# Seven block products instead of eight in the up-projections of a decoder trunk in float32 parts

## The chip, the cores and the metric

The kernel runs on one core of one Trainium2 chip, in one launch. The metric is device time in microseconds (us), lower is better. TensorE (PE) does the matrix products into eight PSUM banks of 128 x 512 float32 numbers, VectorE (DVE) and ScalarE (ACT) do the elementwise work, GpSimd (POOL) a little of it, and SyncE (SP) issues the transfers between main memory and SBUF.

## The reference, cut to what matters

The trunk takes x of 512 tokens by 1024 features and runs two layers. Each layer is a feed-forward block, a mixer (a chunked spatial gating unit in the first layer, sparse attention in the second) and a second feed-forward block, each with a residual and a layer norm. The four feed-forward blocks hold the work that is changed:

```python
def swiglu(x, w1, w3, w2):
    return (jax.nn.silu(x @ w1) * (x @ w3)) @ w2      # w1, w3: 1024 x 2816, w2: 2816 x 1024

h = post_norm(h, 0.5 * swiglu(h, ...), ln_g, ln_b)
```

`x @ w1` and `x @ w3` are the up-projections, the product with `w2` is the down-projection.

## The kernel before, in words

Everything is kept feature-major for the up-projections: `xhi` and `xlo` hold x transposed (1024 features as eight k tiles of 128 partitions, 512 tokens). To keep float32 accuracy each operand is split into two float32r parts: `split` (lines 94 to 96) lets ACT copy the number into the high part and DVE subtract that from the number to give the low part. A product of two split operands takes three matmuls, high by high, high by low and low by high (`three`, lines 162 to 164).

The weights come as units of 128 x 1024 numbers (512 KB) in order of use. The class `Stream` loads a unit into one of two `raw` buffers (line 119, on SP), splits it into `whi` and `wlo` in a ring of five buffers (lines 95 and 96), and hands it out with `take`; `free` gives the buffer back and pumps the next split. One unit of an up-projection is 128 columns of w1 or w3, with all eight k tiles.

`ffn` (from line 261) goes over f = 0 to 21. For each f it makes two products with `feat`, one unit of w1 and one of w3, each of 8 x 3 = 24 matmuls of 512 tokens into a PSUM bank of tag A (tile `pab`), and then `gate` takes Silu on ACT and multiplies on DVE (line 271) into an `h` tile. In the three blocks that follow another layer directly or nearly so, the first four units are run in two halves of 256 tokens, so that TensorE can start before the last tokens have gone through the layer norm. Then `down` runs the token-major product with `w2` (line 236, tile `acc`, eight banks) and, in its last four row tiles, finishes one token tile after the other, each with its layer norm (`ln_tile`, lines 201 to 212), its transposes (line 221) and its split into `xhi` and `xlo`.

The tile framework's scheduler sets the order in which each engine meets its instructions; each engine then works strictly in that order, and waits on semaphores.

Of the kernel before, what the change touches and what calls it, by code (L numbers as in the profile page):

```python
# [17 lines left out]
P = 128  # L18
S = 512
# [20 lines left out]
NRAW = 2  # L40
# [8 lines left out]
NP = 16  # L49
# [5 lines left out]
def trunk_kernel(  # L55
    ctx: ExitStack,
    tc: tile.TileContext,
    x_tok: bass.AP,      # [NT, P, D]
    x_feat: bass.AP,     # [KD, P, S]
    wall: bass.AP,       # [units, P, 1024]  # L60
    lnp: bass.AP,        # [6, 2, D]
    sgu_ln: bass.AP,     # [2, 2, 1024]
    w_s: bass.AP,        # [P(s), 8, P(t)]
    b_s: bass.AP,        # [8, P(t)]
    rel: bass.AP,        # [32, 16]
    onehot: bass.AP,     # [32, S]
    cmp_w1: bass.AP,     # [2, 4, P, 1024]
    cmp_w2: bass.AP,     # [2, P, 2, 128]
    cmp_pe: bass.AP,     # [P, 2, 2, 16]
    cmp_b1: bass.AP,     # [P, 2, 2]  # L70
    out: bass.AP,        # [NT, P, D]
# [5 lines left out]
    work = pool("work", 2)  # L77
# [13 lines left out]
    xhi = const.tile([P, KD, S], F32R, name="xhi")  # L91
    xlo = const.tile([P, KD, S], F32R, name="xlo")
# [5 lines left out]
    # ---------------------------------------------------------------- weights  # L98
    class Stream:
        """Weight units in order of use: loaded ahead, split into two float32r parts ahead.  # L100

        A unit lives in the ring of NB buffers, or, for marked units, in a buffer of the phase's own pool, so that
        the ring can hold units of the next phase before this one ends.
        """

        def __init__(self, n):
            self.n = n
            self.loaded = self.cut = self.taken = self.freed = self.ring = 0
            self.raws, self.units, self.local = {}, {}, {}

        def load(self, upto):
            while self.loaded < min(upto, self.n):
# [12 lines left out]

        def pump(self, n=NB):
# [629 lines left out]
    for k in range(2):  # L756
        split(xhi[:, k, :], xlo[:, k, :], xf[:, k, :])
# [92 lines left out]
```

## Time and profile before

| what | value |
|---|---|
| median of three runs | 2102.51 us (2101.84 to 2107.32) |
| span of the profiled execution | 2100.6 us |
| fastest run less that span | 1.2 us |
| TensorE busy | 2076.1 us, 99% of the span |
| VectorE, ScalarE, GpSimd busy | 45%, 32%, 7% |
| mean granted TensorE clock | 0.996 of full speed |

The profile shows one execution, from its first to its last instruction; the device time of a run holds a little more than this span, here 1.2 us against the fastest run and 1.9 us against the median. The device time of the profiled execution itself is not listed apart. A matmul's duration in the profile includes its way through the array, which overlaps with the next one: what a matmul costs in a stream is the distance from its start to the next start.

### The profile page before, as it was taken

What the parts mean: (1) busy time and instruction counts of PE and PEld (TensorE: products, weight loads), DVE (VectorE), ACT (ScalarE), POOL (GpSimd) and SP (SyncE); (2) the same over time, 40 slices, a digit from 0 to 9 for tenths busy, and PEclk for the clock granted to TensorE, in tenths of its full rate; (3) what the DMA queues carried; (4) which work ended last, traced back from release to release, by engine and by line L of the source; (5) the groups of instructions that cost most, each with busy time, mean ns of one, the idle gap of its engine ahead of it and who ended that gap; (6) DMA issues with size and microseconds to landing.
All of it is one profiled execution on the core that took longest, in us unless ns stands there. A gap on an engine that the chain in (4) does not pass through costs nothing.

```text
span 2100.6 us, 24840 instructions
## 1 busy us (share of the span) xinstructions
PE 2076.1 (99%) x9859; PEld 1720.7 (82%) x9859; DVE 937.0 (45%) x1546; ACT 679.8 (32%) x1062; POOL 139.4 (7%) x249
## 2 busy tenths in 40 slices
PE   9999999999999999999999999999899999999998
PEld 7888888888889888888888888888777788888887
DVE  4322335456447322234733322336688864222234
ACT  4222232333233222222223222222578823222221
POOL 0000000000000000000000000000245500000002
PEclk9999999999999999999999999999899999999999
DMA  6223322333232322323472222222422114322221
GB/s 240 100 91 100 98 93 90 122 129 111 81 114 88 100 94 97 101 93 118 156 273 83 98 100 93 98 100 75 143 66 84 37 41 141 100 94 97 101 93 68
DMA packets 68804, 220.64 MB, mean 105 GB/s; under 512 B 7840, under 2 KB 12192, under 8 KB 67664
## 3 DMA queue, kind: packets, MB, share of 16 engines
q1 hardware_dynamic: 68688, 219.06, 31.3%
q8 instruction: 77, 1.26, 0.2%
q14 instruction: 39, 0.32, 0.0%
HBM read 212.70 MB, written 11.58 MB: 107 GB/s over the span
## 4 chain that ended last, share of the span: by engine, by line
PE 91%; DMA 3%; DVE 2%; ACT 2%; POOL 1%; issue 1%; SPq 0%; DVEq 0%; ACTq 0%; POOLq 0%
PE acc L236 29%; PE pab L162 15%; PE pab L163 15%; PE pab L164 15%; DMA raw<-in_wall_dram 2%; PE pv L163 2%; PE pv L164 2%; PE pv L162 2%; PE pu L164 1%; PE pu L162 1%; PE pu L163 1%; PE pt L658 1%; PE po L668 1%; PE po L669 1%; PE pt L221 1%; PE pss L585 1%
## 5 line engine op out<-in xcount | busy, mean ns | idle before, releaser
L96 DVE TENSOR_TENSOR wlo<-raw,whi 128x1024 fp32r<-128x1024 f32 (+1 forms) x343 | 417.3, 1218 | 518.9 <-ACT whi L95 491.9
L95 ACT ACTIVATE whi<-raw 128x1024 fp32r<-128x1024 f32 (+1 forms) x343 | 359.9, 1052 | 868.9 <-PE pab L163 571.5
L162 PE MATMUL pab<-xhi,whi 128*128 128x512 f32 (+1 forms) x1504 | 565.5, 376 | 0.5 <-ACT xhi L95 0.5
L164 PE MATMUL pab<-xhi,wlo 128*128 128x512 f32 (+1 forms) x1504 | 565.2, 376 | 0.6 <-DVE wlo L96 0.6
L163 PE MATMUL pab<-xlo,whi 128*128 128x512 f32 (+1 forms) x1504 | 565.0, 376 | 0.0
L162 PEld LDWEIGHTS pab<-xhi,whi 128*128 128x128 f32 x1504 | 283.2, 188 | 53.2 <-ACT xhi L95 1.9
L163 PEld LDWEIGHTS pab<-xlo,whi 128*128 128x128 f32 x1504 | 283.2, 188 | 51.9 <-DVE xlo L96 1.0
L164 PEld LDWEIGHTS pab<-xhi,wlo 128*128 128x128 f32 x1504 | 283.1, 188 | 51.6 <-DVE wlo L96 0.8
L236 PE MATMUL acc<-whi,shi 128*128 128x512 f32 x832 | 270.0, 390 | 0.0
L236 PE MATMUL acc<-whi,slo 128*128 128x512 f32 x832 | 269.9, 390 | 0.0
L236 PE MATMUL acc<-wlo,shi 128*128 128x512 f32 x832 | 269.3, 389 | 0.0
L236 PEld LDWEIGHTS acc<-whi,slo 128*128 128x128 f32 x832 | 156.2, 188 | 32.4
L236 PEld LDWEIGHTS acc<-wlo,shi 128*128 128x128 f32 x832 | 156.2, 188 | 32.2
L236 PEld LDWEIGHTS acc<-whi,shi 128*128 128x128 f32 x832 | 156.1, 188 | 31.9
L271 DVE TENSOR_TENSOR h<-tmp,pab 128x512 f32<-128x512 f32 x88 | 60.5, 688 | 272.5 <-PE pab L164 271.8
L96 DVE TENSOR_TENSOR slo<-h,shi 128x512 fp32r<-128x512 f32 x88 | 60.8, 691 | 206.5 <-ACT shi L95 206.5
L188 POOL TENSOR_TENSOR rs<-ve,half_neg 128x1 f32<-128x1 f32 x28 | 26.6, 951 | 1829.1 <-DVE ve L186 1829.1
L95 ACT ACTIVATE shi<-h 128x512 fp32r<-128x512 f32 x88 | 55.5, 631 | 246.2 <-PE acc L236 244.3
L607 POOL TENSOR_SCALAR p<-p,rc,gates 128x128 f32<-128x128 f32 (+3 forms) x128 | 76.4, 616 | 59.3 <-DVE rc L557 29.2
L594 ACT ACTIVATE p<-p,mn 128x128 f32<-128x128 f32 (+3 forms) x128 | 70.8, 554 | 9.8 <-DVE mn L591 9.4
L96 DVE TENSOR_TENSOR tl<-pt,th 128x512 fp32r<-128x512 f32 (+2 forms) x96 | 65.0, 682 | 12.8 <-ACT th L95 10.6
L591 DVE CUSTOM_DVE_ANT_0 p<-pss,u 128x128 f32<-128x128 f32 (+3 forms) x128 | 60.8, 483 | 9.6 <-PE pss L585 4.3
(144 smaller groups left out, 1955.3 us busy)
## 6 DMA issues: line engine op xcount, KB each, us to landing
raw<-in_wall_dram SPq DMA_DIRECT2D x339, 512.0 KB, 3.5
gb<-in_lnp_dram SPq DMA_DIRECT2D x6, 1024.0 KB, 7.5
skew_dr<-rev_dr SPq DMA_DIRECT2D x16, 320.0 KB, 8.2
cw<-in_cmp_w_dram SPq DMA_DIRECT2D x8, 512.0 KB, 6.3
u<-skew_dr SPq DMA_DIRECT2D x16, 256.0 KB, 3.6
k<-k_dr SPq DMA_DIRECT2D x32, 128.0 KB, 3.2
x_sb<-in_x_feat_dram SPq DMA_DIRECT2D x8, 256.0 KB, 5.2
x_sb<-in_x_tok_dram SPq DMA_DIRECT2D x4, 512.0 KB, 6.8
```

The source lines that it names most:

```text
L95: nc.scalar.activation(hi, src, AF.Copy)
L96: sub.tensor_tensor(lo, src, hi.bitcast(F32), op=ALU.subtract)
L162: nc.tensor.matmul(ps, ah, bh, start=first and i == 0, stop=False)
L163: nc.tensor.matmul(ps, ah, bl, start=False, stop=False)
L164: nc.tensor.matmul(ps, al, bh, start=False, stop=last and i == n - 1)
L188: nc.gpsimd.tensor_tensor(rs, ve, half_neg, op=ALU.pow)
L221: nc.tensor.transpose(pt[:, k * P:(k + 1) * P], x_sb[:, t, j * P:(j + 1) * P], ident)
L236: nc.tensor.matmul(acc[t][h], st[:, cs], mv[:, h * 512:(h + 1) * 512], start=s and i == 0, stop=e and i == 2)
L271: nc.vector.tensor_tensor(h, tmp, pb, op=ALU.mult)
L591: nc.vector.tensor_tensor_reduce(out=p[:, :nk], in0=ps[:, m0:m0 + nk], in1=ub[hh][:, S - nk:S], op0=ALU.add, op1=ALU.min, scale=-1.0, scal ...
L594: nc.scalar.activation(p[:, :nk], p[:, :nk], AF.Exp, bias=mn[:, hh:hh + 1], scale=-1.0, accum_out=sm[:, hh:hh + 1])
L607: nc.gpsimd.tensor_scalar(pr[i][:, :nk], pr[i][:, :nk], rc[:, i:i + 1], gates[:, br, h, qt:qt + 1], op0=ALU.mult, op1=ALU.mult)
```

## The change

The first two column pairs of a block (f = 0 and 1, `NPLAIN = 2`) are done as before. The other twenty are done two at a time by `double`. For a pair of columns f the two units (w1 and w3) and x are seen as 2 x 2 blocks: the weights by column (w1, w3) and by half of the features, x by half of the features and half of the tokens. The four block products of 128 columns by 256 tokens that eight smaller products made are now made by seven, after Winograd's form of Strassen's method. Each of the seven has 4 k tiles x 3 matmuls = 12 matmuls of 256 tokens. Sums of weight blocks (`prepare`, four adds of 128 x 512 per column pair, on VectorE) and of x blocks (`combos`, once per block) come before the products, sums of results after them.

`xhi` and `xlo` change their layout to four blocks [feature half + 2 x token half]; after the plain columns, block 2 is overwritten with the x sum `t4`. The ring of five split buffers stays; a `double` uses seven units of it. The raw buffers are two rings of three, by the parity of the unit. The `h`, `r`, `u`, `v`, `p` and `gb` tiles now share one pool of 24 slabs. Layer norms whose result feeds a feed-forward block keep an unsplit transposed copy (`keep`, one more ACT copy per half tile).

```diff
-NRAW = 2
+NRAW = 3
+NSUM = 4
+NSLAB = 24
+NPLAIN = 2
...
+        def plan_double(self):
+            a, b = self.unit, self.unit + 2
+            self.unit += 4
+            self.jobs += [("first", a), ("first", b), ("sum24", a), ("sum24", b), ("sum31", a), ("sum31", b),
+                          ("last", a, b)]
+        def load(self, n=None):
+            while self.loaded < (n or self.unit):
                 i = self.loaded
-                raw = stream.tile([P, 1024], F32, tag="raw", name=f"raw{i}", bufs=NRAW)
+                if i // 2 >= self.retired[i % 2] + NRAW:
+                    return
+                raw = stream.tile([P, 1024], F32, tag=f"raw{i % 2}", name=f"raw{i}", bufs=NRAW)
...
-                if i < 2:
-                    return      # the prologue loads the first two in halves
-                nc.sync.dma_start(raw, wall[i])
+                if i >= 2:
+                    nc.sync.dma_start(raw, wall[i])
...
+            if kind == "first":
+                split(hi, lo, self.raws[u])
+            elif kind == "sum24":
+                a11, a12, a22, a21 = (half(self.raws[u + n], h) for n in range(2) for h in range(2))
+                s31, s24 = self.spare.pop() if self.spare else self.new_sums()
+                nc.vector.tensor_tensor(half(s31, 1), a22, a21, op=ALU.add)
+                nc.vector.tensor_tensor(half(s24, 0), a11, half(s31, 1), op=ALU.add)
+                nc.vector.tensor_tensor(half(s24, 1), a12, half(s24, 0), op=ALU.add)
+                nc.vector.tensor_tensor(half(s31, 0), a11, a21, op=ALU.add)
+                self.sums[u] = s31
+                self.retire(u)
+                split(hi, lo, s24)
+            elif kind == "sum31":
+                split(hi, lo, self.sums.pop(u))
+            else:
+                for h, j in enumerate(of):
+                    split(half(hi, h), half(lo, h), half(self.raws[j + 1], 0))
+                    self.retire(j + 1)
...
+    def combos(x, fp):
+        new = lambda n: [fp.tile([P, 4, 256], F32R, tag=f"x{n}{h}", name=f"x{n}{h}", bufs=1) for h in ("hi", "lo")]
+        t2, t1, t3 = new("t2"), new("t1"), new("t3")
...
+            nc.vector.tensor_tensor(s1, b11, b12, op=ALU.subtract)
+            nc.vector.scalar_tensor_tensor(s2, s1, -1.0, b22, op0=ALU.mult, op1=ALU.subtract)
+            split(t2[0][:, :, cs], t2[1][:, :, cs], s2)
+            split(t1[0][:, :, cs], t1[1][:, :, cs], s1)
+            nc.vector.tensor_tensor(s3, b22, b12, op=ALU.subtract)
+            split(t3[0][:, :, cs], t3[1][:, :, cs], s3)
+            nc.vector.scalar_tensor_tensor(s4, s2, -1.0, b21, op0=ALU.mult, op1=ALU.subtract)
+            t4.append(lambda s4=s4, cs=cs: split(xhi[:, 2, :, cs], xlo[:, 2, :, cs], s4))
...
+    def double(x, hts, fp):
...
+        def product(ps, w, b, start):
+            for k in range(4):
+                for i, (st, mv) in enumerate(((0, 0), (0, 1), (1, 0))):
+                    nc.tensor.matmul(ps, w[st][:, k, :], b[mv][:, k, :], start=start and k == 0 and i == 0,
+                                     stop=k == 3 and i == 2, skip_group_check=True)
+        for s in range(2):
+            product(pp[s], half(first[s], 0), x["b11"], True)
+            nc.scalar.activation(tmp[s][:, 0], pp[s], AF.Copy)
+        for s in range(2):
+            product(qq[s], half(first[s], 1), x["b21"], True)
+            nc.vector.tensor_tensor(tmp[s][:, 0], tmp[s][:, 0], qq[s], op=ALU.add)
+        ws.free(2)
+        s31 = [ws.take() for _ in range(2)]
+        for s in range(2):
+            product(pp[s], half(s24[s], 0), x["t2"], False)
+            nc.scalar.activation(tmp[s][:, 1], pp[s], AF.Copy)
+        for s in range(2):
+            product(rr[s], half(s31[s], 1), x["t1"], True)
+            nc.scalar.activation(tmp[s][:, 2], rr[s], AF.Copy)
+        for s in range(2):
+            product(pp[s], half(s31[s], 0), x["t3"], False)
+            nc.vector.tensor_tensor(tmp[s][:, 2], tmp[s][:, 2], pp[s], op=ALU.add)
+            nc.scalar.activation(hh[s][:, 256:], tmp[s][:, 2], AF.Silu, scale=-1.0)
+        ws.free(2)
+        last = ws.take()
+        for s in range(2):
+            product(rr[s], half(s24[s], 1), x["b22"], False)
+            nc.vector.tensor_tensor(tmp[s][:, 1], tmp[s][:, 1], rr[s], op=ALU.add)
+        ws.free(2)
+        for s in range(2):
+            product(pp[s], half(last, s), x["t4"], False)
+            nc.scalar.activation(hh[s][:, :256], pp[s], AF.Silu, scale=-1.0)
+            nc.vector.tensor_tensor(hh[s], hh[s], tmp[s][:, 0:2].rearrange("p a b -> p (a b)"), op=ALU.mult)
+        ws.free()
...
-    ws.load(1)
-    ws.load(2)
+    ws.load(3)
```

On VectorE, in the middle of the first block's up-projections, two column pairs stood in these rows before (the number in a name is the unit's):

```order
L96 TENSOR_TENSOR wlo32_1104<-raw32_1041,whi32_1103 128x1024
L96 TENSOR_TENSOR wlo33_1139<-raw33_1076,whi33_1138 128x1024
L271 TENSOR_TENSOR h14_1177<-tmp_1175,pab_1144 128x512
L96 TENSOR_TENSOR wlo34_1170<-raw34_1107,whi34_1169 128x1024
L96 TENSOR_TENSOR wlo35_1205<-raw35_1142,whi35_1204 128x1024
L271 TENSOR_TENSOR h15_1243<-tmp_1241,pab_1210 128x512
```

Now two column pairs, one `double`, take 24 rows there. Twelve of them, from the middle of one, follow; the numbers of `wlo` are those of jobs, seven to a `double`, and those of `raw` are the units':

```order
L401 TENSOR_TENSOR tmp_1357<-tmp_1357,q0_1353 128x256
L110 TENSOR_TENSOR wlo37_1414<-sum31_1311,whi37_1413 128x1024
L401 TENSOR_TENSOR tmp_1358<-tmp_1358,q1_1354 128x256
L110 TENSOR_TENSOR wlo38_1418<-raw21_935,whi38_1417 128x512
L110 TENSOR_TENSOR wlo38_1418<-raw23_1177,whi38_1417 128x512
L174 TENSOR_TENSOR sum31_1557<-raw27_1423 128x512
L177 TENSOR_TENSOR sum31_1557<-raw26_1307,raw27_1423 128x512
L175 TENSOR_TENSOR sum24_1558<-raw26_1307,sum31_1557 128x512
L176 TENSOR_TENSOR sum24_1558<-raw26_1307,sum24_1558 128x512
L412 TENSOR_TENSOR tmp_1357<-tmp_1357,p0_1351 128x256
L110 TENSOR_TENSOR wlo39_1510<-raw24_1179,whi39_1509 128x1024
L412 TENSOR_TENSOR tmp_1358<-tmp_1358,p1_1352 128x256
```

The odd units have three raw buffers, so `raw27` lies in the buffer of `raw21`: its transfer can only be issued when the row `wlo38<-raw21` is done, and the first add that reads it stands two rows behind that.

On SyncE, at the start of the program, the order of transfers before was

```order
L739 DMA raw0_116<-in_wall_dram 128x512
L742 DMA x_sb_79<-in_x_feat_dram 128x512 x2
L739 DMA raw1_117<-in_wall_dram 128x512
L742 DMA x_sb_79<-in_x_feat_dram 128x512 x2
```

and is now

```order
L149 DMA raw2_118<-in_wall_dram 128x1024
L909 DMA raw0_116<-in_wall_dram 128x512
L912 DMA x_sb_79<-in_x_feat_dram 128x512 x2
L909 DMA raw1_117<-in_wall_dram 128x512
L912 DMA x_sb_79<-in_x_feat_dram 128x512 x2
```

The whole third unit (512 KB) now goes ahead of the halves and x tiles that the first matmuls read.

On VectorE, at the end of the attention layer, where the last token tile's layer norm (`r30`, `r31`) feeds the last feed-forward block, the rows before were

```order
L202 BN_STATS st_13259<-r31_13261 128x6
L96 TENSOR_TENSOR wlo276_13291<-raw276_13038,whi276_13290 128x1024
L204 BN_AGGR mv_13266<-st_13259 128x2
L96 TENSOR_TENSOR wlo277_13297<-raw277_13068,whi277_13296 128x1024
L186 TENSOR_SCALAR ve_13268<-mv_13266 128x1
L207 SCALAR_TENSOR_TENSOR r30_13260<-r30_13260,mv_13266,gb_9938 128x512
```

and are now

```order
L273 BN_STATS st_16919<-r31_16921 128x6
L174 TENSOR_TENSOR sum31_17206<-raw282_16901 128x512
L275 BN_AGGR mv_16926<-st_16919 128x2
L177 TENSOR_TENSOR sum31_17206<-raw281_16686,raw282_16901 128x512
L251 TENSOR_SCALAR ve_16928<-mv_16926 128x1
L278 SCALAR_TENSOR_TENSOR r30_16920<-r30_16920,mv_16926,gb0_16688 128x512
L278 SCALAR_TENSOR_TENSOR r31_16921<-r31_16921,mv_16926,gb1_16690 128x512
L283 SCALAR_TENSOR_TENSOR x_sb_79<-r30_16920,rs_16930,gb2_16692 128x512
L283 SCALAR_TENSOR_TENSOR x_sb_79<-r31_16921,rs_16930,gb3_16694 128x512
L175 TENSOR_TENSOR sum24_17207<-raw281_16686,sum31_17206 128x512
L110 TENSOR_TENSOR xlo_81<-pt30_16936,xhi_80 128x4x128
L176 TENSOR_TENSOR sum24_17207<-raw281_16686,sum24_17207 128x512
```

The low parts of whole units that stood between the statistics and the normalisation are gone from this place (those of the four plain units now stand ahead of this token tile's sums), and the four adds of a column pair's weight sums stand there instead: two before the normalisation, and two around the first low part of the last token tile.

## Rows read from the trace of the kernel before

**Rows 1.** The page: busy time of each engine, clock, chain, DMA issues.

```profile
span 2100.6 us, 24840 instructions
PE 2076.1 (99%) x9859; PEld 1720.7 (82%) x9859; DVE 937.0 (45%) x1546; ACT 679.8 (32%) x1062; POOL 139.4 (7%) x249
PEclk9999999999999999999999999999899999999999
PE 91%; DMA 3%; DVE 2%; ACT 2%; POOL 1%; issue 1%; SPq 0%; DVEq 0%; ACTq 0%; POOLq 0%
raw<-in_wall_dram SPq DMA_DIRECT2D x339, 512.0 KB, 3.5
x_sb<-in_x_feat_dram SPq DMA_DIRECT2D x8, 256.0 KB, 5.2
```

**Rows 2.** Windows: a block's up-projections, and attention; the last two columns are DMA.

```profile
core 0: us, PE busy (x) PEld busy (x) DVE busy (x) ACT busy (x) POOL busy (x), PEclk, DMA share, GB/s
665.00:892.00 227.00, 227.00 (x1041) 189.69 (x1041) 70.75 (x70) 60.80 (x72) 0.00 (x0) 1.00 0.30 100
1500.00:1690.00 190.00, 182.65 (x989) 140.40 (x988) 157.42 (x569) 152.08 (x403) 98.11 (x190) 0.99 0.19 56
```

**Rows 3.** Groups of TensorE instructions of the up-projections, one line of three.

```profile
L162 PE MATMUL pab<-xhi,whi 128*128 128x512 f32 x1312 | 510.9, 390 | 0.5 <-ACT xhi L95 0.5
L162 PE MATMUL pab<-xhi,whi 128*128 128x256 f32 x192 | 54.6, 285 | 0.0
L162 PEld LDWEIGHTS pab<-xhi,whi 128*128 128x128 f32 x1504 | 283.2, 188 | 53.2 <-ACT xhi L95 1.9
```

**Rows 4.** Timeline of TensorE, 512 columns: start, duration; first and seventh row.

```profile
699.86 0.39 PE L162 MATMUL pab<-xhi,whi 128*128 128x512 f32 x1
...
701.22 0.39 PE L162 MATMUL pab<-xhi,whi 128*128 128x512 f32 x1
```

**Rows 5.** Timeline of TensorE, 256 columns: first and sixteenth row.

```profile
1104.28 0.28 PE L163 MATMUL pab<-xlo,whi 128*128 128x256 f32 x1
...
1106.08 0.28 PE L163 MATMUL pab<-xlo,whi 128*128 128x256 f32 x1
```

**Rows 6.** Groups of VectorE and ScalarE instructions by shape.

```profile
L96 DVE TENSOR_TENSOR wlo<-raw,whi 128x1024 fp32r<-128x1024 f32 x339 | 414.5, 1224 | 515.2 <-ACT whi L95 488.2 <-PE pm L352 20.1
L96 DVE TENSOR_TENSOR slo<-h,shi 128x512 fp32r<-128x512 f32 x88 | 60.8, 691 | 206.5 <-ACT shi L95 206.5
L636 DVE TENSOR_TENSOR o<-po,ol 64x256 f32<-64x256 f32 x32 | 13.3, 416 | 3.7 <-ACT ol L632 3.4
L95 ACT ACTIVATE whi<-raw 128x1024 fp32r<-128x1024 f32 x339 | 357.3, 1057 | 866.6 <-PE pab L163 571.5 <-issue 101.6 <-DMA raw<-in_wall_dram 90.6
L95 ACT ACTIVATE shi<-h 128x512 fp32r<-128x512 f32 x88 | 55.5, 631 | 246.2 <-PE acc L236 244.3 <-DVE h L271 1.9
L594 ACT ACTIVATE p<-p,mn 128x256 f32<-128x256 f32 x32 | 16.0, 501 | 1.8 <-DVE mn L591 1.6
```

**Rows 7.** Timeline of VectorE where its instructions follow each other closely.

```profile
649.92 0.68 DVE L201 SCALAR_TENSOR_TENSOR r<-acc,x_sb 128x512 f32<-128x512 f32 x1
650.52 1.21 DVE L96 TENSOR_TENSOR wlo<-raw,whi 128x1024 fp32r<-128x1024 f32 x1
651.65 1.28 DVE L96 TENSOR_TENSOR xlo<-pt,xhi 128x512 fp32r<-128x512 f32 x2
```

**Rows 8.** Start of the kernel: a window, and first rows of ACT, PE, DVE.

```profile
2.00:10.00 8.00, 7.47 (x21) 3.73 (x20) 4.46 (x7) 4.86 (x9) 0.00 (x0) 1.00 0.94 322
3.59 0.63 ACT L95 ACTIVATE whi<-raw 128x512 fp32r<-128x512 f32 x1 [1.52 <-DMA raw<-in_wall_dram]
5.06 0.79 PE L162 MATMUL pab<-xhi,whi 128*128 128x512 f32 x1
31.06 0.68 DVE L271 TENSOR_TENSOR h<-tmp,pab 128x512 f32<-128x512 f32 x1
```

**Rows 9.** Start of the last block: timelines of VectorE and TensorE.

```profile
1725.77 0.68 DVE L201 SCALAR_TENSOR_TENSOR r<-acc,x_sb 128x512 f32<-128x512 f32 x1
1736.14 1.40 DVE L207 SCALAR_TENSOR_TENSOR r<-r,mv,gb 128x512 f32<-128x512 f32 x2
1740.72 1.28 DVE L96 TENSOR_TENSOR xlo<-pt,xhi 128x512 fp32r<-128x512 f32 x2
1735.01 0.39 PE L164 MATMUL pab<-xhi,wlo 128*128 128x256 f32 x1 [0.56 <-DVE wlo L96]
```

More of the change, by code (lines that the diff above doesn't have):

```diff
@@ L48 @@
 TURN = "BBD"
-NP = 16
 NK = 1
@@ L76, in trunk_kernel @@
     stream = pool("stream", NB)
-    work = pool("work", 2)
+    slabs = pool("slabs", 1)
     small = pool("small", 6)
@@ L137, in pump @@
                 lo = src.tile([P, 1024], F32R, tag="wlo", name=f"wlo{i}", bufs=bufs)
-                for sl in (slice(0, 512), slice(512, 1024)) if i < 2 else (slice(0, 1024),):
-                    split(hi[:, sl], lo[:, sl], raw[:, sl])
+                self.prepare(i, hi, lo)
                 self.units[i] = (hi, lo)
                 self.cut += 1
-                self.load(self.cut + NRAW)
+                self.load()
         def take(self):
@@ new lines, in down, with split_rows, rows @@
+            ln_tile(t, acc[t], c, gb, last, keep)
+    def split_rows(pool, tiles, early=False):
+        def rows(j):
+            if j == 0 and early:
+                hi, lo = (slab("s0").bitcast(F32R) for _ in range(2))
+            else:
+                hi = pool.tile([P, S], F32R, tag="shi", name="shi", bufs=TAIL + 2)
+                lo = pool.tile([P, S], F32R, tag="slo", name="slo", bufs=TAIL + 2)
+            split(hi, lo, tiles[j])
+            return lambda t: (hi[:, t * P:(t + 1) * P], lo[:, t * P:(t + 1) * P])
+        return rows
@@ new lines, in double @@
+    def double(x, hts, fp):
+        first = [ws.take() for _ in range(2)]
+        s24 = [ws.take() for _ in range(2)]
+        half = lambda u, h: [a[:, h * 512:(h + 1) * 512].rearrange("p (k m) -> p k m", k=4) for a in u]
+        pp = [bank("A", f"p{s}")[:, :256] for s in range(2)]
+        qq = [bank("B", f"q{s}")[:, :256] for s in range(2)]
+        rr = [bank("CD"[s], f"r{s}")[:, :256] for s in range(2)]
+        tmp = [fp.tile([P, 3, 256], F32, tag="tmp", name="tmp", bufs=4) for s in range(2)]
+        hh = [slab(f"h{len(hts) + s}") for s in range(2)]
+        hts += hh
+        def product(ps, w, b, start):
[32 more added lines that the diff above has]
+        ws.free()
@@ L275, in ffn, with gate @@
+    def ffn(idx, last=False, first=False, keep=False):
+        hts = []
+        def gate(f, pa, pb):
+            h = slab(f"h{f}")
+            nc.scalar.activation(h, pa, AF.Silu)
+            nc.vector.tensor_tensor(h, h, pb, op=ALU.mult)
+            hts.append(h)
+        with tc.tile_pool(name=f"up{idx}", bufs=2, reuse_waits="tile") as fp:
+            ws.sums_pool = fp
+            ws.spare.append(ws.new_sums())
             if not first:
@@ L369, in sgu @@
                 mix(j)
-            def rows(j):
-                hi = sp.tile([P, S], F32R, tag="shi", name="shi", bufs=TAIL + 2)
-                lo = sp.tile([P, S], F32R, tag="slo", name="slo", bufs=TAIL + 2)
-                split(hi, lo, us[j])
-                return hi, lo
-            down(NSG, rows, 1.0 / ALPHA, gb, half, sp)
+        with tc.tile_pool(name="dnsgu", bufs=2, reuse_waits="tile") as sp:
+            down(NSG, split_rows(sp, us), 1.0 / ALPHA, lnp[idx], sp, keep=True)
     v_dr = dram.tile([P, NT, 1024], F32, name="v_dr")
@@ L721, in nsa @@
                     load_group(i // 8 + 1)
-            down(KD, lambda j: (xhi[:, j, :], xlo[:, j, :]), 1.0 / ALPHA, gb, slab)
+            rows = lambda j: lambda t: tuple(feat_rows(x, j, t * P, (t + 1) * P) for x in (xhi, xlo))
+            down(KD, rows, 1.0 / ALPHA, lnp[idx], keep=True)
     xf = x_sb.rearrange("p t (e c) -> p (t e) c", e=2)
-    zero = const.tile([P, S], mybir.dt.bfloat16, name="zero")
+    zero = slab("zero").bitcast(mybir.dt.bfloat16)[:, :S]
     nc.vector.memset(zero, 0.0)
```

217 lines of the change are left out of this document (135 added, 82 removed).

## Prediction

> **What bounds the kernel now.** The page comes first: TensorE is busy for 2076.1 of 2100.6 us, VectorE for 45%, ScalarE for 32%, and 91% of the chain that ended last is TensorE [rows 1]. The clock row stands at 9 in all but one slice, so nearly the whole span runs at the upper of the two levels, 2.4 GHz [rows 1]. The windows say where that could differ: in the up-projections of the second block TensorE is busy 227.00 of 227.00 us, VectorE 70.75, ScalarE 60.80, with 100 GB/s of transfers; only attention has some 7 us in which TensorE is idle, and there VectorE is busy 157 of 190 us [rows 2]. So in the stage that is changed TensorE alone sets the time, and two thirds of VectorE's time is free there. What matters next is the price of a matmul in a stream. The mean durations, 390 ns for 512 columns and 285 for 256 [rows 3], hold each matmul's way through the array, which lies beside the next one, so distances between starts have to be read: six steps from 699.86 to 701.22 us, **226.7 ns** each, for 512 columns [rows 4], and fifteen steps from 1104.28 to 1106.08 us, **120 ns** each, for 256 columns [rows 5]. Half the columns cost 53% of the time: the narrower form loses 6.7 ns a matmul. Each of these matmuls has a weight load of its own, 188 ns in its record [rows 3], and TensorE still starts one every 120 ns, so the loads pass beside the matmuls.
>
> Before, twenty columns f of a block are 40 units of 24 matmuls: 960 x 226.7 ns = 217.6 us.
>
> **What is removed and added on TensorE.** Now they are ten doubles of 14 products of 12 matmuls: 1680 x 120 ns = 201.6 us, or 20.16 us per double in place of 21.76. That is -16.0 us a block, and **-64 us** in four blocks (exactly seven eighths of eight products would give -27 a block; the 6.7 ns take 11 of it). The plain four units, the down-projections and the attention keep their matmuls.
>
> On prices of matmuls the Trainium skill ("TensorE: Matmul & The Clock Gate", section Back-to-back issue gap) speaks against this change: it gives some 81 ns a matmul at 128 columns and 131 at 512. A straight line between them, an estimate, puts 256 columns at 98 ns: 1680 x 98 = 165 us against 960 x 131 = 126, so 39 us more per block. The rows of this kernel disagree in size and in slope: 226.7 ns where the page has 131 [rows 4], and 120 at half the columns [rows 5].
>
> **What VectorE must do in 20.16 us.** One double has 24 rows there: six of 128 x 1024 (six whole low parts), twelve of 128 x 512 (eight adds of weights, two half low parts, two gates) and six of 128 x 256 (adds of results). Before, two column pairs were four of 1024 and two of 512. Where its instructions follow each other closely, VectorE starts the next one 0.60 us after one of 512 columns and 1.13 us after one of 1024 (649.92, 650.52, 651.65) [rows 7]; 256 columns are not there as such, and I take 0.35 us from the 416 ns of 64x256 less the same overlap of some 0.07 [rows 6]. That is 6 x 1.13 + 12 x 0.60 + 6 x 0.35 = 16.1 us, 80% of a double. By whole durations, 1.224, 0.691 and 0.416 us [rows 6], as where each waits for the one before, it is 18.1 us, 90%. The truth lies between, nearer to the lower end, since only two of the four adds of a group need the add just ahead. ScalarE has six copies of 1057 ns, two of 631 and ten of at most 501 [rows 6]: 12.6 us, 63%. Neither reaches TensorE's 20.16.
>
> **The new wait.** Four units per double are 2.1 MB in 20.16 us, 104 GB/s, as before. But of the odd units only three buffers exist: the transfer of an odd unit (`raw27` in the listing) can be issued when VectorE has read the old one (`wlo38<-raw21`), and the first add that needs it stands two rows later on VectorE. One other half split of 0.60 us lies between. A unit lands a median 3.5 us after its issue [rows 1], so VectorE idles about 3 us in each double, and behind that add stand all later work of VectorE: the add L412 whose PSUM bank the last products write again, and the next low parts. The loop of VectorE is therefore 16.1 - 0.6 + 3.5 = 19.0 us, still under 20.16, and I take it as hidden. By whole durations it is 18.1 - 0.7 + 3.5 = 20.9 and would not be (a rival below). A delay within one double is hidden too as long as it is under some 3.4 us: a bank is written again three products after its last one, 36 x 120 ns = 4.32 us, of which the add itself (0.42) and half of a long row ahead of it (0.5) go off.
>
> **What the starts cost.** These are the places where TensorE's work is short and VectorE's is not.
> - Start of the kernel. The first split waits for a transfer, the queue is full at 322 GB/s, and TensorE starts at 5.06 us [rows 8]. Now the third unit, 512 KB, is issued ahead: 512 KB at 322 GB/s is **+1.6 us**.
> - First block: the x sums are eight adds and eight low parts of 128x512 on VectorE, 16 x 0.65 us (between 0.60 and 0.69 [rows 6, 7]) = 10.4 us, and the products of the first double past the fourth need them. The gate of the second column pair, so the end of the plain units, stands near 31 us [rows 8], and the first four products take another 48 x 120 ns = 5.8. Part of the sums can run beside the plain units, and I allow **+1**.
> - Second block: two of the extra rows ahead of its last layer norm and the sums behind it, **+2**. Third block: its x is ready well ahead, 0.
> - Last block. VectorE is already late there: TensorE waits 0.56 us for a low part, and from the sum at 1725.77 to the last low parts at 1740.72 VectorE has no pause that is worth naming [rows 9]. The order puts four adds around the normalisation (4 x 0.60 = 2.4 us), and two low parts of plain units that stood behind it stand ahead of it (2 x 1.13 = 2.3). The sum of these, 4.7, is nearly all on the path, since TensorE needs this tile for the second halves of its plain units: **+4.5**, with 0 and +8 as ends (nothing of it; the x sums' first adds behind it too).
> - The other layers: attention's slabs share a pool now and its list is ordered anew; its 7 us of idle time could move by some 4 either way [rows 2]. The gate in place, and the extra copies `keep` (eight of 0.63 us on ScalarE per block, beside matmuls) cost nothing while ScalarE is at a third. 0.
>
> Together +9. Sum: 2100.6 - 64 + 9 = 2045.6 us of span. The median of the runs shown is 1.9 us above this profile's span, so **2047 us**.
>
> **Rivals.**
> 1. *Starts cost more.* If half of the four times 10.4 us of x sums is uncovered, some 21 us in place of the 1 to 2 above, it is 2066; if all of it is, 2047 + 41 = 2088. For it: VectorE's crowd at the last block's start [rows 9]. Against: TensorE has four plain units (96 x 2 x 120 ns = 23 us) at each start to cover it. Chance 0.17.
> 2. *VectorE's buffer loop becomes the bound.* At 20.9 us per double it is 0.74 x 40 = 30 us more, less 3.4 of slack once a block: +16, 2063. If a unit lands only after 5.2 us, as the x tiles do where the queue holds other transfers [rows 1], the loop is 18.1 - 0.7 + 5.2 = 22.6: +98 - 14 = +84, **2131**, slower than before. It decides from 21.9 us per double on, since 40 x (21.9 - 20.16) - 14 is the 55 us that the sum has gained; by whole durations that is a landing time of 4.5 us. For it: even units are freed in the same row group, so two transfers can run side by side. Against: 3.5 is a median in a kernel whose two raw buffers also load close together. Chance 0.12 for the first size, 0.05 for the second.
> 3. *Weight loads do not hide.* If a matmul of 256 columns had to wait out its load of 188 ns [rows 3], a block would be 1680 x 188 = 316 us against 217.6, +98, and the kernel 2047 + 4 x (316 - 201.6) = 2505. Already 130 ns a matmul (217.6 / 1680) would eat the gain. Against it: 120 ns with those same loads, in the plain first units [rows 5]. Chance 0.02. The Trainium skill (same page, Part 3, The mechanism) has loads overlap running matmuls only where they aim at other rows of the array, or at the spare weight buffer; with the 188 ns that would be this case, and rows 3 with rows 5 side by side show the overlap.
>
> **How the numbers follow.** The forecast as worked out has 0.64, rival 1 0.17, rival 2 0.17, rival 3 0.02. Its own range is 2036 (starts cost nothing, attention 2 us better) to 2056 (the starts at their upper ends). The lower half of rivals 1 and 2 lies in 2056 to 2084. Range **2036 to 2084**: it leaves out the full size of rival 1, the second size of rival 2 and rival 3, together 0.15, and a few in a hundred below. A measurement of this kernel can tell 0.3%, 6.3 us, from no change: faster means under 2096.2, which all but rival 2's second size, rival 3 and a mixture of the two first rivals reach. Faster 0.92, same 0.03, slower 0.05.
>
> **What the profile after should show.** In the doubles, matmuls of 256 columns (L393) that start every 0.120 us, and 20.2 us from one double to the next, TensorE without pause. VectorE busy for 80 to 90% of the up-projections, idle ahead of L174 for 2 to 3 us a double with the raw transfer as releaser, and TensorE not waiting on it. TensorE idle only at the starts of the blocks, most at the last. The prediction is wrong if starts in the doubles are over 0.13 us apart, if doubles take over 21 us with pauses that end with VectorE or a raw transfer, or if the starts together cost more than some 20 us.

## The result, and the profile after

The changed kernel takes **2036.29 us** (median of four runs, 2035.48 to 2036.93) against 2102.18 us before (four runs): a ratio of 0.9688, 95% interval 0.9674 to 0.9703. The forecast was 2047 us; the range 2036 to 2084 holds the result at its very edge, and two of the four runs lie below it. The profiled execution has a span of 2034.2 us, 66.4 less than before [rows 1], where the sum of the prediction had 55.

The page of the changed kernel, its busy times, clock and chain:

```profile
span 2034.2 us, 32073 instructions
PE 2009.0 (99%) x12739; PEld 1804.4 (89%) x12739; DVE 1383.7 (68%) x2330; ACT 940.5 (46%) x1598; POOL 144.4 (7%) x249
PEclk9999999999999999999999999999999999999999
PE 95%; ACT 2%; DVE 1%; POOL 1%; issue 0%; DMA 0%; SPq 0%; DVEq 0%; ACTq 0%; POOLq 0%
raw<-in_wall_dram SPq DMA_DIRECT2D x339, 512.0 KB, 3.5
```

VectorE has gone from 45% to 68% and ScalarE from 32% to 46%, and the chain still belongs to TensorE. The windows show the stage that was changed, the doubles of the second block (columns as in [rows 2]):

```profile
665.00:865.00 200.00, 200.00 (x1669) 200.00 (x1669) 163.54 (x237) 111.77 (x182) 0.00 (x0) 1.00 0.32 109
```

TensorE has no pause in these 200 us; VectorE is busy for 82% and ScalarE for 56%. The timeline of TensorE gives the length of a double: the first matmul of the last pair of products, in the first double and in the ninth of this block:

```profile
680.65 0.28 PE L393 MATMUL p<-xhi,whi 128*128 128x256 f32 x1
680.77 0.28 PE L393 MATMUL p<-xlo,whi 128*128 128x256 f32 x1
...
841.93 0.28 PE L393 MATMUL p<-xhi,whi 128*128 128x256 f32 x1
```

From 680.65 to 841.93 lie eight doubles of 20.16 us, and a matmul starts 0.12 us after the one before. To see where the 66.4 us come from, the span is cut at the first matmul of the whole program and at the first of each down-projection (tile `acc`), in both timelines of TensorE:

| stretch, by its first matmuls | before | after | difference |
|---|---|---|---|
| start, to the first product | 5.06 | 7.46 | +2.40 |
| first block's up-projections | 241.59 | 225.87 | -15.72 |
| down-projection, gating unit | 312.75 | 314.77 | +2.02 |
| gating unit's down-projection, second up-projections | 332.90 | 316.87 | -16.03 |
| down-projection, shared keys and values, third up-projections | 449.28 | 431.28 | -18.00 |
| down-projection, attention | 329.18 | 324.51 | -4.67 |
| attention's down-projection, last up-projections | 302.50 | 285.98 | -16.52 |
| last down-projection | 127.34 | 127.46 | +0.12 |

The four stretches with up-projections give 66.3 us, some 64 of them by the matmuls; what is left is spread over stages whose matmuls did not change. (The differences add up to -66.40. Each column is one execution; how far a stretch moves from one execution to the next is taken up below, with attention.)

### The profile page after: what moved, and what is told of

Its sections match the earlier page's. It is cut to its first block, busy times and chain, and to the rows that moved or that the text cites. A ratio compares the mean times of both kernels' runs of the same rounds, so it can differ in the third digit from the quotient of the medians.

```text
span 2034.2 us, 32073 instructions
## 1 busy us (share of the span) xinstructions
PE 2009.0 (99%) x12739; PEld 1804.4 (89%) x12739; DVE 1383.7 (68%) x2330; ACT 940.5 (46%) x1598; POOL 144.4 (7%) x249
## 4 chain that ended last, share of the span: by engine, by line
PE 95%; ACT 2%; DVE 1%; POOL 1%; issue 0%; DMA 0%; SPq 0%; DVEq 0%; ACTq 0%; POOLq 0%
PE acc L311 30%; PE p L393 23%; PE r L393 11%; PE q L393 6%; PE pv L227 2%; PE pv L226 2%; PE pv L225 2%; PE pab L226 2%; PE pab L225 2%; PE pab L227 2%; PE pu L226 1%; PE pu L225 1%; PE pu L227 1%; PE pt L819 1%; PE po L829 1%; PE po L830 1%
## 5 line engine op out<-in xcount | busy, mean ns | idle before, releaser
L110 DVE TENSOR_TENSOR wlo<-raw,whi 128x1024 fp32r<-128x1024 f32 (+1 forms) x343 | 370.1, 1092 | 150.9 <-ACT whi L109 111.3
L110 DVE TENSOR_TENSOR wlo<-sum,whi 128x1024 fp32r<-128x1024 f32 x160 | 194.9, 1221 | 21.4 <-ACT whi L109 21.3
L109 ACT ACTIVATE whi<-sum 128x1024 fp32r<-128x1024 f32 x160 | 168.7, 1058 | 87.6 <-PE q L393 35.7
L110 DVE TENSOR_TENSOR slo<-h,shi 128x512 fp32r<-128x512 f32 x84 | 56.4, 691 | 186.9 <-ACT shi L109 186.9
L393 PE MATMUL p<-xhi,whi 128*128 128x256 f32 x640 | 181.3, 283 | 0.0
L393 PE MATMUL p<-xhi,wlo 128*128 128x256 f32 x640 | 181.1, 283 | 0.0
L393 PE MATMUL p<-xlo,whi 128*128 128x256 f32 x640 | 181.1, 283 | 0.0
L174 DVE TENSOR_TENSOR sum<-raw 128x512 f32<-128x512 f32 x80 | 54.9, 687 | 102.0 <-DMA raw<-in_wall_dram 93.8
L393 PEld LDWEIGHTS p<-xhi,whi 128*128 128x128 f32 x640 | 122.8, 192 | 0.2
L393 PEld LDWEIGHTS p<-xlo,whi 128*128 128x128 f32 x640 | 122.9, 192 | 0.0
L393 PEld LDWEIGHTS p<-xhi,wlo 128*128 128x128 f32 x640 | 122.9, 192 | 0.0
L393 PE MATMUL q<-xlo,whi 128*128 128x256 f32 x320 | 90.6, 283 | 0.0
L393 PE MATMUL r<-xt1hi,whi 128*128 128x256 f32 x320 | 90.6, 283 | 0.0
```

The costliest lines, as they stand in the source:

```text
L109: nc.scalar.activation(hi, src, AF.Copy)
L110: sub.tensor_tensor(lo, src, hi.bitcast(F32), op=ALU.subtract)
L174: nc.vector.tensor_tensor(half(s31, 1), a22, a21, op=ALU.add)
L393: nc.tensor.matmul(ps, w[st][:, k, :], b[mv][:, k, :], start=start and k == 0 and i == 0, stop=k == 3 and i == 2, skip_group_check=True)
```

## The experiments

### Eight products in the narrow form

```diff
-                    feat(ps, ws.take())
+                    u = ws.take()
+                    for c0 in (0, 256):
+                        feat(ps, u, c0, c0 + 256)
```

This edit is made to the kernel before.

> The kernel before, with eight block products as ever, but each plain unit behind the first four of a block run in two halves of 256 tokens (48 matmuls in place of 24). Theory A, the price of the form: what the seven products win is 12.5% of the columns, and 256 columns cost 120 ns a start wherever they stand, so 40 units x 48 x 120 ns = 230.4 us against 217.6 per block, +12.8 us, and +51 us in four blocks: 2153 us. Rival B, that the narrower form costs nothing by itself in a dense stream and the gain of the change is what is left of an eighth after work on VectorE: within 6 us of before, 2102.

Measured: 2157.22 us, ratio to before 1.0244 (1.0229 to 1.0260), +52 us on the 2105.19 us of before on the same chip. The timeline has the same 120 ns, fifteen steps from 699.81 to 701.61 us:

```profile
699.81 0.28 PE L163 MATMUL pab<-xlo,whi 128*128 128x256 f32 x1
...
701.61 0.28 PE L163 MATMUL pab<-xlo,whi 128*128 128x256 f32 x1
```

Theory A holds. By these prices the change is two effects: cutting into 256 columns costs +51 us, which this run shows, and leaving out the eighth product saves 4 x (230.4 - 201.6) = 115, which is worked out.

### Four more rows on VectorE, and with one more raw buffer

```diff
-            self.jobs += [("first", a), ("first", b), ("sum24", a), ("sum24", b), ("sum31", a), ("sum31", b),
+            self.jobs += [("first", a), ("first", b), ("sum24", a), ("sum24", b, 4), ("sum31", a), ("sum31", b),
...
+                for n in range(of[1] if len(of) > 1 else 0):
+                    t = half((s31, s24)[n % 2], n // 2 % 2)
+                    nc.vector.tensor_tensor(t, t, t, op=ALU.max)
                 self.sums[u] = s31
```

> The changed kernel with four more additions of 128 x 512 on VectorE per double, in place on the sums (a maximum of a number with itself, so the numbers stay), 2.4 us by starts. Theory A, the loop through the odd raw buffer: 19.0 us of VectorE and transfer per double, so 21.4 with the four rows, 1.24 us over TensorE's 20.16; 40 x 1.24 less some 14 us of slack is +36 us on 2036, about 2072, and TensorE pauses with VectorE or the raw transfer ahead of it. Rival B, no such loop, VectorE's own time alone counts: 16.3 + 2.4 = 18.7 us fit in 20.16, within 4 us of 2036.

Measured: 2042.24 us (2041.72 to 2047.60), ratio to before 0.9705 (0.9689 to 0.9720). Its window of the doubles:

```profile
665.00:865.00 200.00, 200.00 (x1669) 199.99 (x1668) 185.60 (x278) 109.42 (x183) 0.00 (x0) 1.00 0.32 104
```

TensorE still has no pause with VectorE at 93%. The three later blocks are as long as without the rows (316.88, 431.30 and 285.96 us in the stretches of the table); of the 11.7 us by which this execution's span (2045.9) is longer, 7.0 stand in the first block, where TensorE waits 2.70 us for an x sum and then runs at a granted clock of 0.50 from 41.2 to 47.8 us, and 4.6 in attention, where the granted clock is low for longer too (see attention, below). This is the slowest of the four runs; the others are 5.3 to 5.9 us below it. Rival B holds in the doubles, and the median lies 2 us above what it gave. One reservation: the scheduler moved the waiting adds in this kernel. Four rows of VectorE now lie between the half split that frees an odd buffer (L110 at 758.30 us) and the add that waits for the next unit in it (L174 at 762.36), where one did, so the wait of the loop shrank with the work that was added.

The kernel with the fourth odd buffer adds to the four rows:

```diff
-NSLAB = 24
+NSLAB = 23
...
-                if i // 2 >= self.retired[i % 2] + NRAW:
+                if i // 2 >= self.retired[i % 2] + NRAW + i % 2:
...
-                raw = stream.tile([P, 1024], F32, tag=f"raw{i % 2}", name=f"raw{i}", bufs=NRAW)
+                raw = stream.tile([P, 1024], F32, tag=f"raw{i % 2}", name=f"raw{i}", bufs=NRAW + i % 2)
```

> The four more rows per double, and a fourth buffer in the ring of the odd raw units (and 23 in place of 24 slabs, for the room). Theory A: with the fourth buffer the transfer is issued one double earlier, the wait of some 2.4 us per double on VectorE goes, and 16.3 + 2.4 = 18.7 us of work are hidden again: 2036 to 2040 us, and the up-projections back at 20.16 us a double. Rival B, VectorE is bound by its whole durations (18.1 + 2.8 = 20.9): still some 16 us above 2036, 2052, whatever the buffers.

Measured: 2048.23 us, ratio 0.9725 (0.9709 to 0.9742). The doubles are at 20.16 us again, as they were without the buffer; VectorE's wait for raw transfers ahead of L174 fell from 93.8 us in the changed kernel (41.2 with the four rows) to 11.0, and TensorE gained nothing. The time above 2036 lies in the first block (231.74, with the same wait of 2.70 us and a granted clock of 0.50 from 39.8 to 46.5 us), in pauses of 0.8 us at each down-projection of a feed-forward block and in attention (327.10). So the median is nearer to rival B's 2052 than to theory A's 2040, but not by rival B's account, which has longer doubles. The wait was real, and it was hidden.

### Eight more rows

The same edit with 8 in place of 4.

> Eight more additions of 128 x 512 on VectorE per double (four cost nothing in the doubles). Theory A, VectorE binds when its rows by starts pass TensorE's 20.16 us: with four rows it was busy 185.6 of 200 us, with none 163.5, so 22 us more for 9.9 doubles or 0.56 us a row; 16.4 + 8 x 0.56 = 20.9 us per double, 0.7 over, so 40 x 0.7 less 14 us of slack, and some 6 to 10 at the first block as with four rows: 2056 us (2046 to 2075). Rival B, whole durations: 16.4 + 8 x 0.69 = 21.9, 40 x 1.8 - 14 + 8: 2100 us.

Measured: 2090.83 us (2086.97 to 2091.56), ratio 0.9940 (0.9920 to 0.9959). Now VectorE binds. Its window, and two of TensorE's pauses, two doubles apart:

```profile
680.00:880.00 200.00, 193.10 (x1555) 189.29 (x1554) 195.60 (x300) 99.20 (x168) 0.00 (x0) 0.99 0.29 98
```

```profile
755.50 0.39 PE L396 MATMUL r<-xt1hi,whi 128*128 128x256 f32 x1 [0.45 <-ACT whi L109]
...
798.09 0.39 PE L396 MATMUL r<-xt1hi,whi 128*128 128x256 f32 x1 [0.44 <-ACT whi L109]
```

A double takes (798.09 - 755.50) / 2 = 21.30 us, in which VectorE is busy for 195.60 / 200 x 21.30 = 20.8 us and waits for the other 0.5. Those 20.8 are the 16.1 us by starts of the prediction and eight rows of 0.60 [rows 7]; whole durations, 18.1 and eight of 0.69, would make 23.6. (Without the rows VectorE was busy for 163.54 / 200 x 20.16 = 16.5 us a double, its rows less close to each other.) The mechanism is that of theory A, but 2090.83 lies outside its range and nearer to rival B's 2100: its 20.9 us of work were right, and it left out the 0.5 of waits and took off 14 us of slack, of which little shows. The releaser named is ScalarE's split, which itself waits for VectorE's sum.

### One pair after the other, and short gaps

```diff
-            self.jobs += [("first", a), ("first", b), ("sum24", a), ("sum24", b), ("sum31", a), ("sum31", b),
-                          ("last", a, b)]
+            for u in (a, b):
+                self.jobs += [("first", u), ("sum24", u), ("sum31", u), ("last", u)]
...
         for s in range(2):
+            first, s24, s31, last = (ws.take() for _ in range(4))
             product(pp[s], half(first, 0), x["b11"], True)
...
+            product(pp[s], half(last, 0), x["t4"], False)
```

> The changed kernel with its two column pairs one after the other instead of interleaved (the seven products of one pair, then those of the other; the half units of the last product in two ring buffers). A bank is then written again one product (1.44 us) after its last one, not three (4.32 us). Theory A, the interleaving is what hides the readers of the banks: ScalarE's copy can stand behind a split of 1.06 us, VectorE's add behind rows of 1.2 us, the four adds (2.4 us) or the raw transfer (2.4 us), so TensorE pauses 1 to 3 us a pair, 80 pairs: +80 to +240 us on 2036, 2116 to 2276. Rival B, the readers come quickly enough since the order on their engines follows the products: under +10, 2046.

Measured: 2039.51 us (2036.26 to 2040.93), ratio 0.9684 (0.9669 to 0.9698), the same as with the interleaving. VectorE's timeline, the add of t3 in two pairs that follow each other:

```profile
742.77 0.42 DVE L406 TENSOR_TENSOR tmp<-tmp,p 128x256 f32<-128x256 f32 x1 [0.80 <-PE p L391]
743.67 1.23 DVE L110 TENSOR_TENSOR wlo<-sum,whi 128x1024 fp32r<-128x1024 f32 x1 [0.48 <-ACT whi L109]
...
752.85 0.42 DVE L406 TENSOR_TENSOR tmp<-tmp,p 128x256 f32<-128x256 f32 x1 [0.80 <-PE p L391]
```

A pair takes 10.08 us, half of 20.16. VectorE is waiting for the product when it ends, so the add is done 0.5 us behind it and a gap of 1.44 us is enough. Theory A falls. Here the wait for raw transfers is 3.4 us in all, and nothing was gained by that either. The scheduler may still mix the two pairs in places, so the next run sets the short gaps directly:

```diff
+        for s in range(2):
+            product(rr[s], half(s24[s], 1), x["b22"], False)
+            nc.vector.tensor_tensor(tmp[s][:, 1], tmp[s][:, 1], rr[s], op=ALU.add)
         for s in range(2):
             product(pp[s], half(s31[s], 0), x["t3"], False)
...
-        for s in range(2):
-            product(rr[s], half(s24[s], 1), x["b22"], False)
-            nc.vector.tensor_tensor(tmp[s][:, 1], tmp[s][:, 1], rr[s], op=ALU.add)
```

> The changed kernel with one edit in a double: the products with b22 stand ahead of those with t3. Banks r and p are then written again one product (1.44 us) after their last one instead of three (4.32 us), r with ScalarE's copy between, p with VectorE's add. Theory A, the working of the prediction (some 3.4 us of slack come from the three products): VectorE's add stands behind rows of up to 1.2 us, and TensorE pauses by 0.2 to 1 us twice a double: +16 to +80 us on 2036. Rival B, as the run with one pair after the other suggests: VectorE and ScalarE are ahead of TensorE and wait for each product in place, the add is done 0.5 us behind it, and doubles stay at 20.16 us: 2034 to 2040.

Measured in one run: 2044.88 us, span 2043.1. The four stretches with up-projections are longer by 1.7, 2.6, 1.9 and 1.3 us, 7.5 in all; the rest is attention (+1.6). Of the 2.6, 1.7 are not the gaps: behind the gating unit's pauses the granted clock is 0.50 there for 3.4 us, where it was 1.00 in the changed kernel.

```profile
552.00:555.30 3.30, 3.30 (x8) 2.62 (x9) 2.85 (x5) 1.79 (x4) 0.00 (x0) 0.50 0.00 1
```

That leaves 5.8 us, 0.14 a double. Neither theory has the size: the gaps cost something, far less than A has.

### The starts: x sums, order of the first transfers

```diff
-                t1, t2, t3, t4 = combos(x32, fp)
...
-            x = dict(b11=blk(0), b21=blk(1), b22=blk(3), t1=t1, t2=t2, t3=t3, t4=blk(2))
+            x = dict(b11=blk(0), b21=blk(1), b22=blk(3), t1=blk(0), t2=blk(1), t3=blk(3), t4=blk(2))
```

> The changed kernel without the x sums: the products read blocks of x as they stand, so eight adds and eight splits per block (10.4 us on VectorE, 5 on ScalarE) are left out. Theory A, the sums stand beside the plain units and the first products and cost nothing: within 2 us of 2036. Rival B, the rival of the prediction that some of the four times 10.4 us is on the path: 5 to 20 us faster, 2016 to 2031.

Measured: 2036.06 us (2034.32 to 2036.39), ratio 0.9676 (0.9660 to 0.9693). Theory A holds: 41.6 us of VectorE's work in four blocks cost nothing that shows.

```diff
-    ws.load(3)
+    ws.load(2)
```

> The changed kernel with the third unit's transfer issued behind the halves of the first two units and the x tiles, as before the change. Theory A: the first split of weights, which now starts at 5.54 us in place of 3.59, and TensorE, which starts at 7.46 in place of 5.06, come back by the 512 KB at 322 GB/s (1.6 us) and a little more, since TensorE's first matmuls now stand 0.43 us apart: -1.6 to -2.6 us, 2034. Rival B: the first block has a later limit (its x sums on VectorE), so the earlier start is waited away again: 0.

Measured: 2038.59 us (2037.33 to 2039.36), ratio 0.9690 (0.9674 to 0.9706): not faster; the ratio is that of the changed kernel within its interval. TensorE did start at 5.55 us in place of 7.46, and then stood here:

```profile
37.04 0.50 PE L393 MATMUL r<-xt1hi,whi 128*128 128x256 f32 x2 [1.83 <-ACT xt1hi L109]
38.09 0.54 PE L393 MATMUL r<-xt1lo,whi 128*128 128x256 f32 x1 [0.54 <-DVE xt1lo L110]
```

The first down-projection starts at 235.28 us against 233.33. The first block has a second limit, the x sums on VectorE: TensorE comes to the first product that needs them at 35.2 us in place of 37.23, and waits until 37.04. Rival B holds, with a loss on top. Behind these waits the granted clock is 0.50, where it was 1.00 at the same place in the changed kernel:

```profile
38.20:41.50 3.30, 3.30 (x16) 3.30 (x17) 3.30 (x7) 1.26 (x2) 0.00 (x0) 0.50 0.60 168
```

Sixteen matmuls stand in these 3.3 us, against 30 in the changed kernel. VectorE's rows stand in another order too; what that costs by itself was not tried.

### The gating unit's first split

```diff
-            down(NSG, split_rows(sp, us), 1.0 / ALPHA, lnp[idx], sp, keep=True)
+            down(NSG, split_rows(sp, us, True), 1.0 / ALPHA, lnp[idx], sp, keep=True)
```

> The changed kernel with the first split of the gating unit's rows in two slabs, as in the feed-forward blocks, in place of a pool that opens only when the mixer's has closed. Theory A: TensorE's three pauses of 1.0, 0.8 and 0.9 us at the start of that down-projection, which the kernel before did not have, shrink: -1 to -2 us, 2034.5. Rival B: VectorE's eight gates there (0.6 to 0.7 us each) are what is late and not the tile: 0.

The three pauses in question, in the changed kernel's timeline of TensorE:

```profile
546.16 1.16 PE L516 MATMUL pm<-wst,v 128*128 128x128 f32 x8 [0.99 <-DVE m L519]
548.10 0.73 PE L311 MATMUL acc<-whi,shi 128*128 128x512 f32 x2 [0.78 <-ACT shi L109]
...
550.15 0.74 PE L311 MATMUL acc<-whi,slo 128*128 128x512 f32 x2 [0.85 <-DVE slo L110]
```

and the same place with the edit:

```profile
542.75 1.84 PE L516 MATMUL pm<-wst,v 128*128 128x128 f32 x15
544.73 0.74 PE L311 MATMUL acc<-whi,s 128*128 128x512 f32 x2
545.31 0.63 PE L311 MATMUL acc<-wlo,s 128*128 128x512 f32 x2
545.78 1.05 PE L516 MATMUL pm<-wst,v 128*128 128x128 f32 x8
546.59 0.70 PE L311 MATMUL acc<-whi,s 128*128 128x512 f32 x2
```

Measured: **2032.29 us** (2032.23 to 2032.78), ratio to before 0.9661 (0.9645 to 0.9676), 4 us below the changed kernel and the fastest of all. The matmuls of the down-projection stand between those of the mixing again and no pause is left. The stretch is 311.96 us, against 314.77 in the changed kernel and 312.75 before, so 2.8 us are this edit's; TensorE also started 0.5 us earlier in this execution. Theory A holds, a little larger than expected.

### Eight products in quarters

The edit of the first experiment with `for c0 in (0, 128, 256, 384)` and 128 columns.

> The kernel before with eight products, each plain unit behind the first four of a block in four quarters of 128 tokens: what a second level of the same method would have to use. Theory A, a matmul costs its columns and some 13 ns (226.7 = 512 / 2.4 + 13, 120 = 256 / 2.4 + 13), so 128 columns cost 66 ns: 40 x 96 x 66 ns = 255 us against 217.6 a block, +37, 2252 in all. Rival B, at 128 columns the weight loads no longer hide (their records are 188 ns, two can lie beside each other at most): 94 ns or more a matmul, 40 x 96 x 94 = 361 us, +143 a block, 2676 or more.

Measured in one run: 3397.05 us. Two windows, the first in the first block, the second in the third:

```profile
100.00:300.00 200.00, 200.00 (x940) 200.00 (x939) 18.10 (x19) 15.12 (x19) 0.00 (x0) 0.50 0.08 27
1500.00:1700.00 200.00, 200.00 (x1793) 200.00 (x1793) 29.47 (x28) 24.70 (x29) 0.00 (x0) 1.00 0.16 51
```

and the timeline of TensorE in the third block:

```profile
1479.73 0.28 PE L164 MATMUL pab<-xhi,wlo 128*128 128x128 f32 x1
...
1481.41 0.27 PE L164 MATMUL pab<-xhi,wlo 128*128 128x128 f32 x1
```

Fifteen steps take 1.68 us: 112 ns a matmul at the full clock, with half the columns of those at 120. And in the first block the granted clock is 0.50, which is 1.2 GHz, with matmuls some 213 ns apart (940 in 200 us). The price is rival B's (94 ns or more) and not theory A's 66, and the clock comes on top. That it is the weight loads which keep the starts this far apart was not tried.

## Why the prediction was right, and where it was not

**TensorE's price, -64 us: right.** The four blocks gained 15.7, 16.0, 16.1 and 16.5 us (for the third, -18.0 less the 1.9 below), where 16.0 was forecast, and doubles are 20.16 us to the hundredth. The estimate by the Trainium skill's figures ("TensorE: Matmul & The Clock Gate", Back-to-back issue gap) would have had the change slower; here 256 columns stay at 120 ns in three kernels. The Trainium skill's statement (same page, Part 3, The mechanism) that loads are pulled ahead of running matmuls where they aim at other rows of the array or at the spare weight buffer agrees with the 188-ns loads [rows 3] beside 120-ns starts.

**VectorE, 16.1 us a double by starts: right.** It was busy for 16.5, and with eight more rows for 20.8 us, which is 16.1 and eight starts of 0.60. Whole durations, the other end of that term, are refuted.

**The new wait, 19.0 us a double, hidden: right in this kernel.** VectorE's timeline has it:

```profile
755.12 0.69 DVE L174 TENSOR_TENSOR sum<-raw 128x512 f32<-128x512 f32 x1 [2.80 <-DMA raw<-in_wall_dram]
...
775.25 0.69 DVE L174 TENSOR_TENSOR sum<-raw 128x512 f32<-128x512 f32 x1 [2.77 <-DMA raw<-in_wall_dram]
```

16.5 + 2.8 = 19.3 us, under 20.16. Kernels without it are no faster. Whether it would bind as a loop was not settled: with more work on VectorE the scheduler put other rows under it. Rival 2 thus did not come, and the point from which it decides was not tried. The 3.4 us of slack behind it is not a matter of three products: one product between two writes of a bank costs some 0.14 us a double, in one run.

**The starts, +9 us: this step failed.** They came to +2.4 at the start of the kernel (1.6 forecast; ScalarE's first split is 1.95 us later; the variants with this order of transfers start at 6.9 to 7.6 us), +0.3 in the first block (where, after a pause of 2.30 us, the granted clock is 0.66 from 7 to 11 us and matmuls start 0.43 us apart), about 0 in the second and -0.5 in the last, where +4.5 was forecast. The last one is the instructive one. VectorE is as late there as I had it: behind the last matmul on `acc`, the last low part of the token tile ends after 16.7 us, against 12.3 before. Before, that is from here to the end of the low parts of 1740.72 [rows 9], at 1742.00:

```profile
1729.73 0.39 PE L236 MATMUL acc<-whi,xlo 128*128 128x512 f32 x1
```

and in the changed kernel from the first of these rows to the end of the second:

```profile
1679.61 0.39 PE L311 MATMUL acc<-whi,xlo 128*128 128x512 f32 x1
1695.61 0.68 DVE L110 TENSOR_TENSOR xlo<-pt,xhi 128x512 fp32r<-128x512 f32 x1
```

That is 4.4 us more, where 4.5 was forecast. But TensorE does not wait, as its timeline shows:

```profile
1693.01 0.28 PE L393 MATMUL q<-xhi,whi 128*128 128x256 f32 x1
1693.14 0.60 PE L292 MATMUL pt<-ident,x_sb 128*128 128x128 f32 x4
1693.49 0.36 PE L393 MATMUL q<-xlo,whi 128*128 128x256 f32 x1
1693.69 0.28 PE L393 MATMUL q<-xhi,wlo 128*128 128x256 f32 x1
1693.81 0.60 PE L292 MATMUL pt<-ident,x_sb 128*128 128x128 f32 x4
```

These rows on `q` are the first double's products with b21, the first 256 tokens of x. They need nothing of the last token tile, so the scheduler set them between the halves of the plain units, around the last transposes. Two of a double's seven products work on that token half alone: the change brought cover of its own, and I had counted only the plain units' second halves behind the layer norm. This cover is twelve matmuls, 1.4 us. The rest of the delay fell into room that the kernel before already had: by count, the 96 matmuls of its plain units' first halves last until 14.3 us behind the last on `acc`, 2 us more than the 12.3 that it needed. So the step that failed is "nearly all on the path". This is read from the timelines; no run takes the cover away. Nor is TensorE idle most at the last block, as the prediction had it: 0.12 us there, against 11 in attention.

**What I had at 0 elsewhere.** The gating unit lost 2.0 us, by a pool that opens later (shown by the edit that takes it away). Between the second and third block 1.9 us were gained: TensorE's wait of 1.8 us for a transfer (`cw`) is gone in the group of line L620.

**Attention, 4.7 us gained, where I gave it 4 either way.** Most of it is the granted clock, which the prediction left out here. In the profiled execution before, TensorE runs two stretches of attention at 0.50, which is 1.2 GHz, each behind a pause (3.40 us for a transfer of `k`, 1.92 us for `pc`):

```profile
1486.53 0.47 PE L583 MATMUL pss<-k,qs 128*128 128x160 f32 x1 [3.40 <-DMA k<-k_dr]
1485.10:1491.80 6.70, 5.27 (x14) 4.24 (x15) 3.52 (x4) 3.87 (x5) 0.22 (x1) 0.50 0.78 216
1498.80:1505.50 6.70, 6.70 (x22) 5.22 (x22) 4.96 (x26) 5.23 (x18) 1.75 (x4) 0.50 0.26 82
```

In that of the changed kernel it is one shorter stretch, behind a pause of 1.25 us:

```profile
1609.20:1612.50 3.30, 3.30 (x12) 2.66 (x13) 3.30 (x11) 1.82 (x6) 2.38 (x5) 0.50 0.02 5
```

Half of the busy time in these stretches, 6.0 us before and 1.7 after, is an estimate of what the lower level cost; all pauses of attention together are 12.6 us before and 11.2 after. The nine kernels with the changed attention code say the same: their attention takes 323.9 to 324.7 us in the five that have some 3.4 us at 0.50, 326.1 and 327.1 with 6.8, 327.8 with 10.2 and 329.1 with 13.7, and their pauses differ by 1.4 us at most. The three kernels with the old attention code (before, and the two experiments on it) have 6.8 to 13.7 us at 0.50 and take 326.8 to 329.2 us. How much of the 4.7 is the kernel's and how much the two executions' that were profiled is therefore open; it is not the products'. The device time moves with the clock in the same way: in seven runs of the kernel before on one chip the span goes from 2098.5 us at a mean clock of 0.998 to 2106.8 at 0.994.

So the forecast's mechanism held, and 2047 was 11 us too high by the starts (9 in place of 2.2) and by attention's 4.7; the gating unit's 2.0 and the 1.9 behind the second block nearly cancel. That the range still holds the result, by 0.3 us, owes something to luck: its lower end stood for starts that cost nothing and 2 us of gain in attention, and the starts did cost 2.2 while attention gave 4.7.

## What to carry to other kernels

Price a cut into more, smaller matmuls by the distance between starts at the new width, from rows of the same kernel: here 512, 256 and 128 columns cost 226.7, 120 and 112 ns, so one level of seven for eight pays and a second, on 128 columns, would not by these prices (no run tries it). Work that is added to a second engine is free until its rows, by starts, fill the first engine's period: 16.5 of 20.16 us cost nothing, 18.7 cost nothing in the steady state, 20.8 and short waits, 21.3 in all, set the time. Put the granted clock beside a stretch before two executions of it are compared. Before a start is charged, look in the order for products that need only the part of the input which is ready, and look at pools that open late in stages that were only moved: that one cost as much as the whole start of the kernel.

## What the hardware showed that I had not expected

Matmuls of 128 columns start 112 ns apart at the full clock, nearly as far as those of 256 (120 ns), each with a weight load of 0.19 us in the record. The same stream ran at a granted clock of 0.50 in nearly all of the first block (940 matmuls in 200 us) and at 1.00 in the third (1793): TensorE was busy for 200 of 200 us in both windows, so the busy row alone does not tell the two apart. The lower level ended at 913 us, when matmuls of the down-projection, 512 columns wide, had run since 908.82:

```profile
8.90:913.20 904.30, 904.27 (x4228) 902.99 (x4228) 81.30 (x83) 68.99 (x83) 0.00 (x0) 0.50 0.10 33
913.40:1000.00 86.60, 86.60 (x383) 71.65 (x383) 30.79 (x33) 26.38 (x33) 0.00 (x0) 1.00 0.31 100
```

This is one execution; what holds the clock down in that stretch was not tried.
